# A task of the side work that wakes from a pause goes on only at every second group of weights

## The chip, the cores and the metric

The kernel runs on one core of one Trainium2 chip. The metric is the device time of one execution in microseconds (us). The profile is of one execution; its engines are PE (TensorE; PEld is its weight load), DVE (VectorE), ACT (ScalarE), POOL (GpSimd) and SP, whose queue issues nearly all the DMAs.

## What is computed

One inference step of a decoder with two layers, for 256 prompt tokens and 8 sequences of 4 new tokens, all in float32. Cut to what matters here, a layer is:

```python
g_cols, u_pool, u_conf, u_sc, q, k, v, qi, ki, wi = split_cols(x @ w_in)
a_out = pool_mixer(u_pool, ...)                       # sums over 2, 4, 8, 16 rows, then a small matmul
b_out = silu(layer_norm(causal_dwconv(ga * sigmoid(gb), ...)))     # 31 taps
c_out = sb * causal_dwconv(sc_ * sh, ...)             # 3 taps
d_out = attend(q, k, v, qi, ki, wi)                   # top-k of an indexer's scores, softmax over those keys
gates = sigmoid(g_cols)
merged = (gates[0] * (a_out @ w_br_pool) + gates[1] * (b_out @ w_br_conv)
          + gates[2] * (c_out @ w_br_sconv) + gates[3] * (d_out @ w_br_attn))
x1 = layer_norm(ALPHA * x + merged @ w_o)
r = ALPHA * x1 + (silu(hg) * hu) @ w_ffn_out          # hg, hu = x1 @ w_ffn_in
y = layer_norm(r + (pe @ w_pe) * sigmoid(r @ w_pg))
```

The attention of the prompt (`attn_prompt`) and that of the new tokens (`attn_sample`), which reads pages of a cache of keys and values, together give `d_out`.

## The kernel before

Activations lie with features on the partitions: a tile of 128 features x 288 columns (256 prompt tokens and 32 new ones). A weight matrix is cut into tiles of 128x128, and eight of them, in the order of their use, make a **group** of 512 KB. There are 306 groups. Each weight is split into a rounded high part and a rest, and so is each activation; a tile of weights costs three matmuls (lines 292 to 294): high x high, high x rest, rest x high. A group is thus 24 matmuls of PE.

**The pipeline of the groups.** When PE's program comes to a new group g, `W` (line 278) calls `fetch`: SP issues the DMA of group g+5 into `wraw` (4 buffers), ACT makes `whi` of group g+3 (line 264, 4 buffers), DVE makes `wlo` of group g+2 (line 271, 3 buffers).

**The side work.** Behind `fetch`, `W` calls `side`, which advances a counter, `tick`, and lets the tasks go on. A task is a Python generator that emits instructions: `conv`, `sconv`, `pool`, `index_prompt`, `index_sample`, `attn_prompt`, `attn_sample`. The instructions stand in each engine's order where the generator emitted them, all at this point between two groups. A task yields a pair (microseconds of DVE, of ACT), which is taken from the budget of this tick (1.96 and 2.3 us), or a whole number n, a **pause**: it goes on n ticks later at the earliest. The task does so where its next instruction needs the result of another engine, and also where it waits for a buffer of `b` or a bank `ax`. `conv` alone is low: it goes on where no other task can. Each engine works through its own order strictly, so what the side work emits on PE stands between the matmuls of two groups.

**Where a task must be done.** `layer` calls `finish` for a task whose result comes next. It steps that task until it is done, and at every advance of the tick each other task too that has no pause left, with no budget and with no group of weights in between. In a layer the order around this is: `qkv`, the projections for the other mixers, gates 0 and 2, `finish(pool)`, branch pool, `finish(sconv)`, branch sconv, gates 1 and 3 (16 projections of 8 weight tiles: one group each), then `finish` of the index and attention tasks, `pe_load` (a DMA, then a split by ACT at line 327 and DVE at line 328), branch attn, `finish(conv)`. A branch takes 4 groups and its outputs are multiplied by a gate on DVE (lines 1057 and 1060), out of 4 PSUM buffers `mm`.

**The end of the attention tasks**, which the prediction follows. `attn_prompt`, second block: scores masked (line 837) and their maximum (842), eight Exp on ACT (849), normalised on DVE (856), four rounds of four transposes on PE (868), each copied by ACT (870), the product with the values (880), copied by ACT (884), its rest on DVE (887). `attn_sample`, second half (f = 1): pages of keys by 8 DMAs of 256 KB (913) into `kv`, scores on PE (976, 979, 983), maximum on DVE (988), 8 DMAs for the values, Exp (994), three transposes (1002, 1003), copied by ACT (1005, 1006), the product with the values (1011, 1014), scaled on DVE (1018), four small matmuls that gather the heads (1027), copied by ACT (1032), the rest on DVE (1035). Both write `dp`, which the first matmul of branch attn reads.

Of the kernel before, what the change touches and what calls it, by code (L numbers as in the profile page):

```python
# [109 lines left out]
class Task:  # L110
    def __init__(self, gen, low):
        self.gen, self.wake, self.done, self.low, self.needs = gen, 0, False, low, BOTH


class Builder:
# [74 lines left out]
    def step(self, t):  # L190
        try:
            r = next(t.gen)
        except StopIteration:
            t.done = True
            self.tasks.remove(t)
            return
        if isinstance(r, int):
            t.wake = self.tick + r
        elif r is VECTOR or r is BOTH:
            t.needs = r  # L200
        else:
            self.left[0] -= r[0]
            self.left[1] -= r[1]

    def side(self):
        self.tick += 1
        for i in range(2):
            self.left[i] = min(self.left[i], 0.0) + self.budget[i]
        can = lambda t: not t.done and t.wake <= self.tick and all(self.left[i] > 0 for i in t.needs)
        while True:  # L210
            ready = [t for t in self.tasks if can(t)]
            if not ready:
                break
            ready = [t for t in ready if not t.low] or ready
            for t in ready:
                if can(t):
                    self.step(t)
# [674 lines left out]
    def load_kidx(self):  # L892
        nc, l, d = self.nc, self.l, self.d
        self.kx = self.sb.tile([128, 4, 2, 128], F32, name="kv", tag="kv", bufs=4)
        rows = slice(PHYS * l, PHYS * (l + 1))
        for b in range(NB):
            for g in range(2):
                i = 2 * b + g
                if i not in self.page:
                    self.page[i] = nc.sync.value_load(self.pt[0:1, i:i + 1], min_val=0, max_val=PHYS - 1)  # L900
                nc.sync.dma_start(self.kx[64 * (b % 2):64 * (b % 2) + 64, b // 2, g],
                                  d["kidx"][rows][ds(self.page[2 * b + g], 1)].rearrange("a p k -> p (a k)"))
                yield 0, 0.01
            yield 1

    def load_pages(self, which, f):
        nc, l, d = self.nc, self.l, self.d
        rows = slice(PHYS * l, PHYS * (l + 1))
        out = []
        for b in range(4 * f, 4 * f + 4):  # L910
            t = self.sb.tile([128, 2, 4, 128], F32, name="kv", tag="kv", bufs=4)
            for g in range(2):
                nc.sync.dma_start(t[:, g].rearrange("p c k -> p (c k)"),
                                  d[which][rows][ds(self.page[2 * b + g], 1)].rearrange("a p k -> p (a k)"))
            out.append(t)
        yield 1
        return out

    def index_sample(self):
# [520 lines left out]
```

## Time and profile before

| | |
|---|---|
| time, median of 3 runs | 1084.68 us (1083.91 to 1085.72) |
| the profiled execution | 1083.62 us, of which the span of the trace is 1081.8 us |
| PE busy | 1066.2 us, 99% of the span |
| PE weight load busy | 1030.5 us, 95% |
| DVE, ACT, POOL busy | 770.9, 557.5, 174.4 us (71%, 52%, 16%) |
| DMA | 188.58 MB, 174 GB/s |

A matmul's shown time is that of its way through the pipeline; what a matmul costs is the distance between two starts. The number in brackets behind a row is the idle time of its engine just ahead of it, and what ended it. Lines are those of the kernel before; in the changed kernel the lines named here and below stand 6 lower (line 880 is 886 there).

### The profile page before, as it was taken

To read this page: it belongs to the slowest core of one execution; us is meant where nothing else is said; L and a number is where in the kernel's file an instruction comes from. 1 tells how busy PE (TensorE), PEld (TensorE's weight loads), DVE (VectorE), ACT (ScalarE), POOL (GpSimd) and SP (SyncE) were. 2 spreads that over 40 slices of the span, in tenths; PEclk is the share of its full clock that TensorE was granted. 3 is DMA by queue.
4 is the path that set the end of the run, shared out by engine and by line. 5 is a ranking of instruction groups with operands and counts; after the bars stand their busy time and mean duration, and the time that the engine had idled before them with its cause. 6 is when DMAs were issued, how large, how long until landed. Compare 5 with 4: busy or idle time off the path is not lost.

```text
span 1081.8 us, 20642 instructions
## 1 busy us (share of the span) xinstructions
PE 1066.2 (99%) x8138; PEld 1030.5 (95%) x8138; DVE 770.9 (71%) x1305; ACT 557.5 (52%) x930; POOL 174.4 (16%) x175
## 2 busy tenths in 40 slices
PE   9999999999999999999999999999999999999996
PEld 8999989999999999999999998899999999999995
DVE  5898858678785555545789897687698765555456
ACT  5866445455564444434578565363545644443334
POOL 0720003005500000000437100030055000000004
PEclk9999999999999999999999999999999999999998
DMA  9476566344445555554445856563453644554541
GB/s 320 153 260 205 180 238 212 115 163 150 153 156 176 156 172 169 166 160 166 167 151 176 283 175 211 195 212 119 152 168 118 196 159 163 173 171 159 173 137 44
DMA packets 61732, 188.58 MB, mean 174 GB/s; under 512 B 7587, under 2 KB 12227, under 8 KB 61635
## 3 DMA queue, kind: packets, MB, share of 16 engines
q1 hardware_dynamic: 60498, 183.54, 51.5%
q0 software_dynamic: 992, 3.57, 0.9%
q8 instruction: 64, 1.05, 0.4%
q14 instruction: 34, 0.27, 0.1%
q10 hardware_dynamic: 144, 0.15, 0.1%
HBM read 182.48 MB, written 4.75 MB: 173 GB/s over the span
## 4 chain that ended last, share of the span: by engine, by line
PE 91%; DVE 4%; ACT 2%; POOL 2%; issue 1%; DMA 0%; SPq 0%; DVEq 0%; POOLq 0%; ACTq 0%
PE mm L292 24%; PE mm L293 24%; PE mm L294 24%; PE mm L319 2%; PE mm L321 2%; PE mm L315 2%; DVE wlo L271 1%; PE ax L293 1%; PE ax L292 1%; PE ax L294 1%; PE ax L321 1%; POOL b L341 1%; PE ax L319 1%; PE ax L315 1%; POOL b L372 1%
## 5 line engine op out<-in xcount | busy, mean ns | idle before, releaser
L271 DVE TENSOR_TENSOR wlo<-wraw,whi 128x1024 fp32r<-128x1024 f32 (+1 forms) x309 | 384.4, 1246 | 144.6 <-issue 79.6
L292 PE MATMUL mm<-xh,whi 128*128 128x288 f32 x1536 | 455.3, 296 | 0.8 <-DVE s L1060 0.8
L294 PE MATMUL mm<-xh,wlo 128*128 128x288 f32 x1536 | 453.1, 295 | 0.9 <-DVE wlo L271 0.8
L293 PE MATMUL mm<-xl,whi 128*128 128x288 f32 x1536 | 453.2, 295 | 0.0
L264 ACT ACTIVATE whi<-wraw 128x1024 fp32r<-128x1024 f32 (+1 forms) x309 | 322.6, 1046 | 152.3 <-PE mm L293 80.7
L292 PEld LDWEIGHTS mm<-xh,whi 128*128 128x128 f32 x1536 | 288.8, 188 | 8.6 <-issue 7.4
L294 PEld LDWEIGHTS mm<-xh,wlo 128*128 128x128 f32 x1536 | 288.6, 188 | 1.7 <-DVE wlo L271 1.6
L293 PEld LDWEIGHTS mm<-xl,whi 128*128 128x128 f32 x1536 | 288.8, 188 | 0.4
L292 PE MATMUL mm<-b,whi 128*128 128x288 f32 x576 | 171.8, 298 | 0.0
L293 PE MATMUL mm<-b,whi 128*128 128x288 f32 x576 | 169.9, 295 | 0.0
L294 PE MATMUL mm<-b,wlo 128*128 128x288 f32 x576 | 169.5, 294 | 0.0
L292 PEld LDWEIGHTS mm<-b,whi 128*128 128x128 f32 x576 | 107.9, 187 | 0.9 <-issue 0.4
L294 PEld LDWEIGHTS mm<-b,wlo 128*128 128x128 f32 x576 | 108.5, 188 | 0.0
L293 PEld LDWEIGHTS mm<-b,whi 128*128 128x128 f32 x576 | 108.1, 188 | 0.3
L1061 POOL TENSOR_TENSOR m<-m,s 128x288 f32<-128x288 f32 x32 | 38.2, 1226 | 273.5 <-DVE s L1060 273.5
L339 POOL TENSOR_TENSOR b<-xf 128x288 f32<-128x288 f32 x4 | 4.9, 1220 | 443.5 <-DVE xf L1206 434.8
L1179 ACT ACTIVATE b<-s 128x288 fp32r<-128x288 f32 x44 | 19.3, 445 | 92.1 <-DVE s L1174 92.1
L682 DVE SCALAR_TENSOR_TENSOR b<-b,prm 128x256 f32<-128x256 f32 x120 | 63.1, 573 | 0.0
L1174 DVE TENSOR_TENSOR s<-s,mm 128x288 f32<-128x288 f32 x40 | 18.0, 454 | 50.4 <-PE mm L294 50.4
L1045 ACT ACTIVATE xf<-mm 128x288 f32<-128x288 f32 x32 | 13.2, 412 | 63.0 <-PE mm L294 63.0
L1045 ACT ACTIVATE g<-mm 128x288 f32<-128x288 f32 x32 | 13.2, 412 | 60.2 <-PE mm L294 60.1
L1182 DVE TENSOR_TENSOR b<-s,b 128x288 fp32r<-128x288 f32 x44 | 19.8, 458 | 19.4 <-ACT b L1179 19.4
(252 smaller groups left out, 1235.1 us busy)
## 6 DMA issues: line engine op xcount, KB each, us to landing
wraw<-in_w_dram SPq DMA_DIRECT2D x304, 512.0 KB, 3.5
kv<-in_ck_dram SPq DMA_DIRECT2D x32, 256.0 KB, 5.3
kv<-in_cv_dram SPq DMA_DIRECT2D x32, 256.0 KB, 4.8
out_ko_dram<-b POOLq DMA_DIRECT2D x2, 576.0 KB, 5.0
out_vo_dram<-b POOLq DMA_DIRECT2D x2, 576.0 KB, 7.2
kv<-in_kidx_dram SPq DMA_DIRECT2D x32, 32.0 KB, 3.1
b<-in_p_dram SPq DMA_DIRECT2D x3, 288.0 KB, 4.0
wraw<-in_w_dram SPq DMA_DIRECT2D x3, 256.0 KB, 4.8
```

The source lines that it names most:

```text
L264: self.nc.scalar.activation(self.hi[g][:, c[i]], self.raw[g][:, c[i]], AF.Copy)
L271: self.nc.vector.tensor_tensor(self.lo[g][:, c[i]], self.raw[g][:, c[i]], self.hi[g][:, c[i]].bitcast(F32), op=OP.subtract)
L292: m(out, wh, rh, start=first, stop=False)
L293: m(out, wh, rl, start=False, stop=False)
L294: m(out, wl, rh, start=False, stop=last)
L315: m(o, wh, rh[:, k], start=k == 0, stop=False)
L319: m(o, wh, rl[:, k], start=False, stop=not early and k == nk - 1)
L321: m(o, wl, rh[:, k], start=False, stop=False)
L682: nc.vector.scalar_tensor_tensor(o, e, wj, o, op0=OP.mult, op1=OP.add)
L1045: self.nc.scalar.activation(g, a, AF.Sigmoid)
L1061: nc.gpsimd.tensor_tensor(self.m[:, j], self.m[:, j], t, op=OP.add)
L1182: nc.vector.tensor_tensor(h[:, 1, i % 2], t, h[:, 0, i % 2].bitcast(F32), op=OP.subtract)
```

## The change

A pause that ends at an odd tick is lengthened by one tick: a task other than `conv` that has yielded a whole number goes on only at an even one. The same holds for a task that polls for a buffer. A pair as a yield is not touched, and neither is `finish`, which looks at the pause alone. The pauses behind the page DMAs are excepted: they yield 1.0 in place of 1, a float, for which the mark is not set.

```diff
 class Task:
     def __init__(self, gen, low):
         self.gen, self.wake, self.done, self.low, self.needs = gen, 0, False, low, BOTH
+        self.turn = False
...
-        if isinstance(r, int):
-            t.wake = self.tick + r
+        t.turn = isinstance(r, int) and not t.low
+        if isinstance(r, (int, float)):
+            t.wake = self.tick + int(r)
...
-        can = lambda t: not t.done and t.wake <= self.tick and all(self.left[i] > 0 for i in t.needs)
+
+        def can(t):
+            return (not t.done and t.wake <= self.tick and all(self.left[i] > 0 for i in t.needs)
+                    and not (t.turn and self.tick % 2))
...
@@ load_kidx and load_pages
-            yield 1
+            yield 1.0
```

Instructions of the same kinds and sizes stand in another order; two more loads of ACT's function table are the only new ones on a compute engine. On PE the side work stood in 48 places between the weight matmuls and stands in 43 now. Three places follow.

PE, first layer, between gate 3 and branch attn. Rows whose input is `xh` or `xl` are the end of gate 3, rows with input `b` the start of branch attn. Before:

```order
L292 MATMUL mm<-xh,whi 128x288
L293 MATMUL mm<-xl,whi 128x288
L294 MATMUL mm<-xh,wlo 128x288
L292 MATMUL mm<-b,whi 128x288
L293 MATMUL mm<-b,whi 128x288
L294 MATMUL mm<-b,wlo 128x288
```

The same place now:

```order
L298 MATMUL mm<-xh,whi 128x288
L299 MATMUL mm<-xl,whi 128x288
L300 MATMUL mm<-xh,wlo 128x288
L874 MATMUL ax<-const_214,b 128x128 x4
L1008 MATMUL ax<-const_214,rls 128x128 x2
L1009 MATMUL ax<-const_214,rls 32x128
L886 MATMUL ax<-b 64x128 x16
L1017 MATMUL ax<-vs,pst 128x512
L1020 MATMUL ax<-kv,pst 32x512 x8
L1033 MATMUL ax<-const_214,b 128x16 x4
L298 MATMUL mm<-b,whi 128x288
L299 MATMUL mm<-b,whi 128x288
```

The last round of transposes of `attn_prompt` and the whole end of `attn_sample` moved here; they stood 12 to 15 groups earlier. The second layer has the same rows at this place, with eight transposes in place of four and with L886 ahead of L1008.

ACT, second layer, the same place: L1045 (L1051 now) is the sigmoid of a gate, L327 (L333) the split of `pe_load`. Before:

```order
L1045 ACTIVATE g<-mm 128x288
L264 ACTIVATE whi<-wraw 128x1024
L730 ACTIVATE s<-b 128x288 x2
L1045 ACTIVATE g<-mm 128x288
L327 ACTIVATE b<-b 128x576
L264 ACTIVATE whi<-wraw 128x1024
```

Now:

```order
L1051 ACTIVATE g<-mm 128x288
L876 ACTIVATE b<-ax 128x512 x2
L736 ACTIVATE s<-b 128x288
L890 ACTIVATE b<-ax 128x4x128
L736 ACTIVATE s<-b 128x288
L1011 ACTIVATE pst<-ax 128x256
L1012 ACTIVATE pst<-ax 32x128
L1038 ACTIVATE b<-ax 128x4x16
L333 ACTIVATE b<-b 128x576
L270 ACTIVATE whi<-wraw 128x1024 x2
```

The copies that PE's rows at this place need stand between the sigmoid of the last gate and the split, with a sigmoid of `conv` (L736) among them.

ACT, first layer, the eight Exp of the second block of `attn_prompt`. Before, in the branches pool and sconv, where ACT has no gate to work on:

```order
L264 ACTIVATE whi<-wraw 128x1024 x2
L849 ACT_TABLE_LOAD
L849 ACTIVATE b,st<-b,st 128x256 x8
L264 ACTIVATE whi<-wraw 128x1024 x2
L994 ACTIVATE rls,sts<-ax,sts 128x288
```

Now, in gate 1:

```order
L1051 ACTIVATE xf<-mm 128x288
L270 ACTIVATE whi<-wraw 128x1024
L855 ACT_TABLE_LOAD
L855 ACTIVATE b,st<-b,st 128x256 x8
L1051 ACT_TABLE_LOAD
L1051 ACTIVATE xf<-mm 128x288
L270 ACTIVATE whi<-wraw 128x1024
```

They moved 7 groups down the program, out of the branches; in the second layer they move by as much.

## Rows read from the trace of the kernel before

**Rows 1.** The page: busy time of PE, and the chain that ended last, by engine.
```profile
PE 1066.2 (99%) x8138; PEld 1030.5 (95%) x8138; DVE 770.9 (71%) x1305; ACT 557.5 (52%) x930; POOL 174.4 (16%) x175
...
PE 91%; DVE 4%; ACT 2%; POOL 2%; issue 1%; DMA 0%; SPq 0%; DVEq 0%; POOLq 0%; ACTq 0%
```

**Rows 2.** Timeline of PE (start us, us, engine, line): two rows 116 matmuls apart.
```profile
244.78 0.29 PE L293 MATMUL mm<-b,whi 128*128 128x288 f32 x1
...
260.25 0.30 PE L292 MATMUL ax<-b,whi 128*128 128x288 f32 x1
```

**Rows 3.** Timeline of PE: blocks of side work in both layers.
```profile
192.31 1.09 PE L868 MATMUL ax<-const,b 128*128 128x128 f32 x8
...
729.98 0.60 PE L868 MATMUL ax<-const,b 128*128 128x128 f32 x4
730.33 0.39 PE L292 MATMUL mm<-xh,whi 128*128 128x288 f32 x1
730.55 0.30 PE L293 MATMUL mm<-xl,whi 128*128 128x288 f32 x1
...
733.69 1.97 PE L880 MATMUL ax<-b 128*64 128x128 f32 x32
735.59 1.12 PE L1011 MATMUL ax<-vs,pst 32*128 32x512 f32 x2
...
738.50 0.40 PE L292 MATMUL mm<-xh,whi 128*128 128x288 f32 x1
...
741.77 0.96 PE L1027 MATMUL ax<-const,b 128*128 128x16 f32 x8
742.58 0.38 PE L292 MATMUL mm<-xh,whi 128*128 128x288 f32 x1
```

**Rows 4.** Timeline of the other engines: copies and scalings of the attention tasks.
```profile
140.39 0.59 ACT L870 ACTIVATE b<-ax 128x512 f32<-128x512 f32 x1
140.87 0.38 ACT L1005 ACTIVATE pst<-ax 128x256 f32<-128x256 f32 x1
141.13 0.25 ACT L1006 ACTIVATE pst<-ax 32x128 f32<-32x128 f32 x1
...
202.34 0.22 DVE L1035 TENSOR_TENSOR b<-ax,b 128x64 fp32r<-128x64 f32 x1
...
735.71 0.60 ACT L884 ACTIVATE b<-ax 128x512 fp32r<-128x512 f32 x1 [0.55 <-PE ax L880]
738.71 0.75 DVE L1018 SCALAR_TENSOR_TENSOR b<-ax,sts,const 128x512 f32<-128x512 f32 x1 [3.63 <-PE ax L1014]
743.23 0.21 ACT L1032 ACTIVATE b<-ax 128x64 fp32r<-128x64 f32 x1
```

**Rows 5.** Timeline of PE: the pages' first use (first layer, f = 1).
```profile
148.90 0.96 PE L1027 MATMUL ax<-const,b 128*128 128x16 f32 x8
...
161.83 0.75 PE L976 MATMUL ax<-scs,const 32*128 32x288 f32 x2
...
163.52 1.93 PE L983 MATMUL ax<-kv,qbd 128*32 128x256 f32 x32
```

**Rows 6.** The tile kv on SP from 150 to 156 us: its eight DMAs.
```profile
L913 SPq DMA_DIRECT2D kv<-in_ck_dram x8: 332/333/463, 151.0 to 154.8; - x8
DMA to landing us min/median/max: 3.5/5.0/5.4
```

**Rows 7.** Timeline: ends of branch sconv, first and second layer.
```profile
182.11 0.37 PE L292 MATMUL mm<-xh,whi 128*128 128x288 f32 x1 [0.26 <-DVE s L1060]
...
715.32 1.79 DVE L271 TENSOR_TENSOR wlo<-wraw,whi 128x1024 fp32r<-128x1024 f32 x1 [0.42 <-ACT whi L264]
...
718.18 0.37 PE L292 MATMUL mm<-xh,whi 128*128 128x288 f32 x1 [0.58 <-DVE s L1060]
```

**Rows 8.** Windows: stretch, us, busy (xinstructions) by engine, granted clock, DMA share, GB/s.
```profile
1070.00:1074.00 4.00, 2.31 (x34) 1.58 (x34) 2.00 (x6) 2.01 (x6) 1.30 (x3) 1.00 0.01 4
1074.00:1078.00 4.00, 0.33 (x3) 0.13 (x2) 3.74 (x11) 2.97 (x6) 2.65 (x4) 0.51 0.28 100
```

More of the change, by code (lines that the diff above doesn't have):

```diff
@@ L915, in load_pages @@
             out.append(t)
-        yield 1
+        yield 1.0
         return out
```

## The prediction

> **What bounds the kernel now.** I read the page first: PE is busy for 99% of the span, and of the chain that ended last 91% is PE [rows 1]. No other engine is near that. So what counts is what stands in PE's order, and where PE stands still.
>
> Next the pace of that order. Two matmuls of the stream that are 116 apart start 15.47 us apart [rows 2], so one weight matmul costs 0.1334 us, a group of 24 costs 3.20 us, and the 7344 of the program (306 groups) some 980 us. About 100 us of the 1081.8 are left for side work on PE, layer norms, start and end.
>
> Then single blocks of side work. Four transposes hold the stream for 0.35 us (729.98 to 730.33), and the weight matmul behind them takes 0.22 us to the next start in place of 0.13: 0.09 us for leaving a block. The product with the values takes 1.90 us for the prompt (733.69 to 735.59) and 2.91 for the sample (735.59 to 738.50), the four gathering matmuls 0.81 (741.77 to 742.58) [rows 3]. None of these rows carries a wait: ACT's and DVE's answers are ready when PE comes to the next step, because at least one group of 3.2 us lies between.
>
> **The change, part by part.** *Work.* No matmul, and no instruction that computes on DVE or ACT, is added or taken away; two more loads of a function table run on ACT (52% busy [rows 1]) beside the stream. What changes is when a task goes on. A pause that would end at an odd tick costs one group more, and the chain of pauses of an attention task gets longer by many of these. Before, both attention tasks are done some 10 groups before `finish` asks for them, in each layer. Now they aren't, and the rest comes out in one piece, between gate 3 and branch attn. There PE has nothing else in its order. I call this piece the tail.
>
> *The tail, second layer.* I follow PE from the first of the eight transposes (t = 0). Eight are busy for 1.09 us, four for 0.60, so eight hold PE for 0.35 + 0.49 = 0.84 us [rows 3]. ACT has the sigmoid of the last gate ahead (done by then), and two copies of 512 columns: 0.59 us each, the next instruction starting 0.48 later [rows 4]. From an end to a start on another engine I take 0.06 us (the product's last end at 735.66 [rows 3], ACT's copy at 735.71 [rows 4]). First copy from 0.66, second from 1.15 to 1.74, PE on at 1.80, free at 0.84: wait 0.96. The prompt's product takes 1.90, to 3.70, then three transposes about 0.24, to 3.94. ACT copies the product from 3.82, has a sigmoid of `conv` next (an estimate: 0.34, between the 0.26 to the next start of a 256-column copy and the 0.48 of a 512-column one), then the copies of the three transposes, 0.26 and 0.25 [rows 4], done at 5.15, PE on at 5.21: wait 1.27. The sample's product takes 2.91, to 8.12. DVE starts the scaling 0.21 behind that (738.50 to 738.71) and takes 0.75 [rows 3, 4]; PE on at 9.14: wait 1.02. The gathering takes 0.81, to 9.95, its end shows 0.15 later [rows 3]; ACT's copy takes 0.21 and then DVE's rest 0.22 [rows 4]: first weight matmul at 10.4, the second held by 0.15 more: wait 0.63. Together 3.9 us.
>
> *The tail, first layer.* Four transposes and the three of the sample fill 0.59 us; ACT's copy is done at 1.25, PE goes on at 1.31: wait 0.72. ACT copies for the sample while the product runs, so there is no second wait. Scaling and gathering as above: 1.02 and 0.63. Together 2.4 us.
>
> Both tails: 6.3 us. From below: scaling and gathering have no other PE work beside them by the order, 2 x (1.02 + 0.63) = 3.3. From above: every copy in full behind its matmul, none overlapped with PE or with another: 5.4 and 3.6, so 9. I take 6.3, since each piece has its row.
>
> *Behind the tail.* PE's wait holds up branch attn alone. On DVE there queue behind the scaling the rest of dp, the split of `pe_load`, and `wlo` of the group two ahead; that weight is needed 6.4 us after the tail's end, so I cost it at nothing. Without that cover it would be the 1.8 us that such a `wlo` once took [rows 7]. The DMA of `pe_load` stands in SP's queue ahead of weights that are due five groups later.
>
> *The pages of keys, first layer (f = 1).* A block begins at 148.90, at the start of the group ahead of the page DMAs [rows 5]. The last of these is issued at 154.8 and lands at most 5.4 later [rows 6], so 11.3 us behind that group's start. PE needs them at 163.52, 14.6 behind it, because blocks of side work lie between [rows 5]. Now three bare groups do, 9.6 us, and the 1.7 us of lines 976 and 979 (161.83 to 163.52): 11.3. The slack is gone, and the eight Exp of `attn_prompt`, now a few groups earlier in gate 1, may set ACT back, and with it `wlo` and SP. I take 0.5, between 0 and 2. In the second layer blocks still lie between: 0.
>
> *Waits that may go.* At the end of branch sconv PE stands 0.26 us in the first layer and 0.58 in the second, for DVE, which itself stood 0.42 for a late `whi` of ACT [rows 7], behind the eight Exp. These leave this stretch. First layer: DVE has no more beside the branch than before, so -0.35 with the slow restart of 0.09. Second layer: maskings of scores and a maximum move into the branches, and the last step of `pool` stands nearer to its branch: I take no change, between -0.7 and +1.5.
>
> *Fewer blocks.* 43 for 48: five times 0.09 = -0.45, between 0 and -1.0 (if entering costs as much as leaving).
>
> *Sum.* 6.3 + 0.5 - 0.35 - 0.45 = +6.0 us. The profiled execution took 1083.62 us, 1.06 below the median of the three runs; 6.0 on the median gives **1090.7 us** (1089.6 for an execution like the profiled one).
>
> **A rule weighed.** From 1070 to 1074 us PE is busy for 2.31 of 4 us and the granted clock is still 1.00 (2.4 GHz); in the next 4 us, with 0.33 busy, it is 0.51 (1.2 GHz) [rows 8]. In the tails PE works for some 7 of 11 and 6 of 9 us, so by the rows the clock holds. The Trainium skill, "TensorE: Matmul & The Clock Gate", section "Why this matters for your kernels", asks that there be no long idle gaps between bursts of matmuls, since the clock then falls back; it speaks against a chain of waits in one place, and what a fall would give is rival B.
>
> **The rivals.**
> A. *The tail costs only what the order forces.* ACT's copies are done when PE comes to them, so that scaling and gathering alone stall: 3.3 us. With both branch waits gone (-1.0) and the full 1.0 for the blocks the net is +1.3: 1086.0, not slower by what can be told. For it: ACT is idle for half of the span [rows 1]. Against: in the second layer ACT's chain is longer than the PE work beside it, by rows. It decides where the tails come to under 4.2 us and the gains reach their far ends.
> B. *The clock falls in the tails.* At the low level a weight matmul takes twice its 0.133 us. If that lasts for the 4 us of the low window [rows 8], 15 matmuls take 2 us more, at both tails 4: 1094.7. Against it: the window before that.
> C. *DVE's queue becomes the next wait.* Behind the scaling stand a split and a `wlo`; if these hold up the reading of the branch's outputs as in branch sconv now (0.58 [rows 7]), and the pages come late too, that is 1.5 to 3 more: 1093. For it: DVE stands still through much of the tail with its queue behind it.
> D. *The gains outweigh.* Entering and leaving a block costs far more than 0.09, which no row shows. It would take over 1.5 us per block against the tails: 1082.
>
> **How the numbers follow.** About 0.2% (2.2 us) is what a measurement of this kernel can tell from no change. Forecast 0.76, A 0.09, B 0.05, C 0.07, D 0.03. The predicted time is the forecast's, 1090.7. Its unknown terms reach from +1.3 to +12.5; I leave out the ends, where several terms would have to lie at their bounds at once: 1087.0 to 1094.8. Slower: forecast, B and C, less the forecast's lowest part, 0.87; same: A and that part, 0.10; faster 0.03.
>
> **What would show it.** In the trace of the changed kernel: a block of PE between gate 3 and branch attn in each layer, some 9 and 11 us long, with waits of PE for ACT's line 876 (0.7 and 1.0), ACT's 1012 in the second layer (1.3), DVE's 1024 (1.0 each) and ACT's 1038 (0.5 each); no wait of PE at the end of branch sconv in the first layer; at most 2 us of wait for `kv` at line 989 in the first layer; granted clock 1.00 throughout. I am wrong if PE's waits in the tails sum to less than 4.5 us, if a new wait of over 1.5 us stands outside the tails, or if the stream's pace of 0.133 us changes.

## The result, and the profile after

The changed kernel takes 1095.44 us (median of four runs, 1092.84 to 1097.63), the kernel before 1084.51 beside it: a ratio of 1.0098, 95% interval 1.0075 to 1.0122, so slower by 10.9 us. The forecast was 1090.7 in a range of 1087.0 to 1094.8: the direction was right, the size was not. The profiled execution took 1095.4, with a span of 1093.6, which lies at the median. One execution of an experiment below, of 1283.1 us at a mean granted clock of 0.76, is left out of its median. The runs of one kernel lie up to 5.6 us apart, so a difference of two medians below is good to one or two us; the sizes of single places come from the traces.

First the page of the kernel after: busy time by engine, and the chain, as in [rows 1].

```profile
PE 1072.8 (98%) x8138; PEld 1034.2 (95%) x8138; DVE 769.7 (70%) x1305; ACT 561.3 (51%) x932; POOL 174.8 (16%) x175
...
PE 87%; ACT 3%; DVE 3%; DMA 2%; issue 2%; POOL 2%; SPq 1%; POOLq 0%; DVEq 0%; ACTq 0%
```

As many matmuls as before (x8138) and two table loads more on ACT; but PE is busy for 6.6 us longer, and DMA, 0% of the chain before, has 2%. What PE waited for, from the view of waits (instruction, what it waited for: us in all, times, longest):

```profile
PE ax L989 <- DMA kv<-in_ck_dram: 2.0, 3, 0.9
PE ax L1033 <- DVE b L1024: 1.9, 2, 1.0
PE ax L886 <- ACT b L876: 1.2, 1, 1.2
PE ax L1017 <- ACT pst L1012: 1.0, 1, 1.0
...
PE mm L298 <- ACT b L1038: 0.6, 2, 0.3
```

The last four are the tails, at the lines that the prediction named. The first is the pages of keys, to which it gave 0.5 us. The tails themselves, second layer (from the eight transposes) and then first layer, timeline of PE:

```profile
778.28 1.03 PE L874 MATMUL ax<-const,b 128*128 128x128 f32 x8
779.25 0.44 PE L886 MATMUL ax<-b 128*64 128x128 f32 x4
780.84 1.75 PE L886 MATMUL ax<-b 128*64 128x128 f32 x28 [1.15 <-ACT b L876]
...
784.03 1.12 PE L1017 MATMUL ax<-vs,pst 32*128 32x512 f32 x2 [0.96 <-ACT pst L1012]
...
787.95 1.07 PE L1033 MATMUL ax<-const,b 128*128 128x16 f32 x8 [0.95 <-DVE b L1024]
789.33 0.40 PE L298 MATMUL mm<-b,whi 128*128 128x288 f32 x1 [0.31 <-ACT b L1038]
789.59 0.40 PE L299 MATMUL mm<-b,whi 128*128 128x288 f32 x1
789.83 0.29 PE L300 MATMUL mm<-b,wlo 128*128 128x288 f32 x1
```

```profile
240.27 0.60 PE L874 MATMUL ax<-const,b 128*128 128x128 f32 x4
...
240.92 0.27 PE L1009 MATMUL ax<-const,rls 128*32 128x128 f32 x1
241.13 1.97 PE L886 MATMUL ax<-b 128*64 128x128 f32 x32
...
246.95 1.06 PE L1033 MATMUL ax<-const,b 128*128 128x16 f32 x8 [0.95 <-DVE b L1024]
248.33 0.40 PE L298 MATMUL mm<-b,whi 128*128 128x288 f32 x1 [0.31 <-ACT b L1038]
```

Next the product with the pages for f = 1, first layer and second. Before, in the first layer, it was one piece of 1.93 us with no wait [rows 5]; now it stands twice for `kv` and takes 6.0 us, 211.88 to 217.88:

```profile
211.88 1.03 PE L989 MATMUL ax<-kv,qbd 128*32 128x256 f32 x4
213.72 0.99 PE L989 MATMUL ax<-kv,qbd 128*32 128x256 f32 x2 [0.81 <-DMA kv<-in_ck_dram]
214.98 2.97 PE L989 MATMUL ax<-kv,qbd 128*32 128x256 f32 x26 [0.27 <-DMA kv<-in_ck_dram]
217.88 1.24 PE L708 MATMUL ax<-b,const 128*128 128x288 f32 x4
...
760.74 0.63 PE L989 MATMUL ax<-kv,qbd 128*32 128x256 f32 x6
762.25 1.89 PE L989 MATMUL ax<-kv,qbd 128*32 128x256 f32 x26 [0.88 <-DMA kv<-in_ck_dram]
```

And the granted clock (windows; the number behind POOL's is the clock). Before it was 1.00 from start to end, but for the last microseconds [rows 8]:

```profile
212.00:216.00 4.00, 2.92 (x18) 0.96 (x21) 2.50 (x10) 0.00 (x0) 0.00 (x0) 0.72 1.03 412
216.00:220.00 4.00, 4.00 (x34) 2.68 (x26) 0.46 (x1) 0.00 (x0) 0.00 (x0) 0.85 0.42 169
786.00:790.00 4.00, 2.74 (x24) 1.66 (x17) 1.82 (x5) 0.94 (x3) 0.00 (x0) 1.00 0.00 0
790.00:794.00 4.00, 4.00 (x21) 4.00 (x21) 2.24 (x3) 0.80 (x1) 0.80 (x1) 0.58 0.27 74
```

Ahead of its end the program had two falls of the clock to the lower level (1.2 GHz, 0.5): in the wait for the pages, and just behind the second tail, where branch attn is already running: 21 matmuls instead of some 30 in 4 us. Their starts there (timeline of PE):

```profile
791.08 0.45 PE L299 MATMUL mm<-b,whi 128*128 128x288 f32 x1
791.32 0.45 PE L300 MATMUL mm<-b,wlo 128*128 128x288 f32 x1
```

In the pages the fall costs too: the 26 matmuls behind the last landing show 2.97 us in the first layer, and 1.89 in the second, where the clock was 1.00.

**Where the time went.** All kernels here have the same 7344 weight matmuls in the same order, so the start of the n-th in one trace can be subtracted from its start in another. The differences say, group by group, where a kernel falls behind the kernel before. In us, for the changed kernel and three experiments told below:

| stretch (groups of 24 weight matmuls) | after | pages early | no Exp | filled |
|---|---|---|---|---|
| start, 0 to 24 | -0.22 | +0.70 | +0.62 | +1.59 |
| first layer, 24 to 72 | +5.72 | +3.10 | +3.29 | +1.57 |
| of it the group with the pages f = 1 | 8.64 | 4.50 | 4.68 | 4.50 |
| of it the tail, with the group behind it | 8.29 | 9.82 | 9.81 | 8.29 |
| second layer, 168 to 238 | +5.66 | +6.62 | +2.69 | +2.71 |
| of it the group with the pages f = 1 | 5.65 | 4.19 | 4.19 | 4.18 |
| of it the tail, with the group behind it | 12.80 | 15.21 | 11.28 | 11.28 |
| program | +11.24 | +10.45 | +6.61 | +5.91 |

(The lines "of it" hold work that before stands elsewhere, so only their differences from column to column count.) Pages: 8.64 - 4.50 = 4.14 in the first layer, 5.65 - 4.19 = 1.46 in the second, 5.6 in all. The fall of the clock behind the second tail: 12.80 - 11.28 = 1.5. What is left is the tails net of all gains: 5.72 - 4.14 = 1.58 and 5.66 - 1.46 - 1.52 = 2.68, 4.3 in all. With the start's -0.2 that makes 11.2. The 4.14 of the first layer's pages are 3.0 of lateness (the last load lands at 214.84, PE is there at 211.88) and 1.1 of the clock (2.97 - 1.89).

### The profile page after: what moved, and what is told of

Same layout as the page of the kernel before. It is cut to its first block, busy times and chain, and to the rows that moved or that the text cites. A ratio compares the mean times of both kernels' runs of the same rounds, so it can differ in the third digit from the quotient of the medians.

```text
span 1093.6 us, 20646 instructions
## 1 busy us (share of the span) xinstructions
PE 1072.8 (98%) x8138; PEld 1034.2 (95%) x8138; DVE 769.7 (70%) x1305; ACT 561.3 (51%) x932; POOL 174.8 (16%) x175
## 4 chain that ended last, share of the span: by engine, by line
PE 87%; ACT 3%; DVE 3%; DMA 2%; issue 2%; POOL 2%; SPq 1%; POOLq 0%; DVEq 0%; ACTq 0%
PE mm L298 23%; PE mm L299 23%; PE mm L300 23%; PE mm L325 2%; PE mm L327 2%; PE mm L321 2%; DMA kv<-in_ck_dram 1%; PE ax L299 1%; DVE wlo L277 1%; PE ax L298 1%; PE ax L300 1%; PE ax L989 1%; POOL b L347 1%; ACT whi L270 1%; PE ax L327 1%
## 5 line engine op out<-in xcount | busy, mean ns | idle before, releaser
L1051 ACT ACTIVATE g<-mm 128x288 f32<-128x288 f32 x32 | 13.2, 413 | 52.1 <-PE mm L300 52.0
L1051 ACT ACTIVATE xf<-mm 128x288 f32<-128x288 f32 x32 | 13.2, 411 | 42.1 <-PE mm L300 42.1
```

The lines of the kernel that those rows point to most:

```text
L1051: self.nc.scalar.activation(g, a, AF.Sigmoid)
```

## The experiments

**How the pages come late.** ACT in the changed kernel, timeline from a `whi` over the eight Exp of the prompt's second block (their last ends at 197.9) to the next `whi`; then DVE, and SP's eight loads:

```profile
191.57 1.05 ACT L270 ACTIVATE whi<-wraw 128x1024 fp32r<-128x1024 f32 x1
192.64 1.28 ACT L855 ACT_TABLE_LOAD   x1
...
198.01 1.28 ACT L1051 ACT_TABLE_LOAD   x1
199.30 0.41 ACT L1051 ACTIVATE xf<-mm 128x288 f32<-128x288 f32 x1
199.61 1.05 ACT L270 ACTIVATE whi<-wraw 128x1024 fp32r<-128x1024 f32 x1
```

```profile
200.69 1.23 DVE L277 TENSOR_TENSOR wlo<-wraw,whi 128x1024 fp32r<-128x1024 f32 x1 [3.39 <-ACT whi L270]
```

```profile
205.49 4.11 SPq L919 DMA_DIRECT2D kv<-in_ck_dram  x8
```

In the kernel before, the same Exp stood in branch sconv, where ACT has no sigmoid in its queue:

```profile
173.00 1.28 ACT L849 ACT_TABLE_LOAD   x1
...
178.25 1.99 ACT L264 ACTIVATE whi<-wraw 128x1024 fp32r<-128x1024 f32 x2
```

There the Exp held ACT for 5.25 us and two `whi` followed at once. In gate 1 a sigmoid stands between, with a table load of its own: 6.97 us from 192.64 to the next `whi`. The Trainium skill, "ScalarE: Activation LUTs", section "Table sets: the hidden batching unit", has it that functions come in sets and that changing the set costs a load; the trace agrees, at 1.28 us each. `wlo` needs `whi`, the buffer of raw weights is free only behind `wlo`, and SP's weight loads wait for that buffer with the loads of `kv` behind them: last issue 209.27, landing 4.1 to 5.6 us after the issue, the last at 214.84, while PE is there at 211.88. Theory: late pages and tails cost, and the clock falls behind such waits. Two experiments take the pages' lateness away in different ways.

*Pages early.* In `attn_sample`:

```
             nc.tensor.matmul(...)                 # last readers of kv for f = 0
+            if not f:
+                early = self.pages("ck", 1)       # eight DMAs issued here
...
-                kt = yield from self.load_pages("ck", f)
+                kt = early
+                yield 1.0
```

> The changed kernel, but the eight DMAs for the second half's pages of keys are put into SP's queue right behind the matmuls that read the buffers last (the values of the first half), some 10 groups earlier; the order on PE, ACT and DVE is unchanged. Theory 1 (two causes: late pages cost about 4.2 us in the first layer and 1.6 in the second with the fall of the clock that follows them, the tails some 6 us and 1.6 for the clock): no wait for the pages is left, the two blocks that hold them fall from 8.6 and 6.4 us to about 4.4 and 4.7, the tails stay at 8 and 11 us, the time falls by 5 to 6 us, to 1089 to 1090.5. Rival (the pages are late because DMA bandwidth is short there, and what is moved away comes back as late weights): the time falls by less than 2 us and PE waits for wlo instead.

Measured: 1091.17 (1088.32 to 1093.96), ratio 1.0057 (1.0036 to 1.0078), 4.3 us less than the changed kernel. No wait for `kv` is left, and the group with the pages costs 4.14 and 1.46 us less in the two layers. The profiled execution, the longest of the four, shows why no more came of it (windows over the second tail):

```profile
784.00:788.00 4.00, 2.86 (x16) 1.78 (x8) 1.49 (x3) 0.18 (x2) 0.00 (x0) 0.50 0.00 0
788.00:792.00 4.00, 3.90 (x16) 3.90 (x17) 2.58 (x4) 1.57 (x3) 0.00 (x0) 0.50 0.16 26
```

Here the clock fell inside the tail and stayed at 0.50 into branch attn: 15.21 us in place of 11.28. It fell behind the first tail as well: 9.82 in place of 8.29. Over its four runs the mean granted clock and the time go together: 0.997 twice (1088.3, 1089.4), 0.993 (1092.9), 0.991 (1094.0). So the tails net of the gains, without a fall of the clock, cost some 4 us.

*No Exp.* In `attn_prompt`, both layers:

```
-            for h in range(8):
+            if i:
+                nc.vector.memset(st[:, 1], 1e30)  # row sums of the second block
+            for h in range(8 if i == 0 else 0):
```

> The changed kernel without the eight Exp of the second block of the prompt's attention, in both layers (the sums of the rows are set to a constant, so the output isn't the reference's); the order of all else is unchanged. Theory 1 (in the first layer the Exp, now in gate 1, make ACT late with whi, so DVE with wlo, so SP with the weights that stand ahead of the pages): SP issues the pages some 2 us earlier against PE, PE's wait for them in the first layer falls from about 3.6 us to under 1.5 and the clock stays up there; the second layer, where the Exp lie further ahead, keeps its wait of 1.5. The time falls by 2.5 to 4.5 us, to 1091 to 1093. Rival (the distance of two bare groups alone is too short for the burst of eight DMAs, whatever ACT does): the wait stays over 2.5 us and the time within 1.5 us of the changed kernel.

Measured: 1090.38 (1089.10 to 1092.93), ratio 1.0063 (1.0045 to 1.0080), 5.1 us less. No wait for `kv` in either layer; in the first the loads go out from 203.4 on, in an execution whose stream stands 0.84 later there, so 2.9 us earlier against the stream than in the changed kernel; in the second they go out 1.8 us earlier against it. The product with the pages is one piece again:

```profile
212.72 2.11 PE L991 MATMUL ax<-kv,qbd 128*32 128x256 f32 x32
```

That settles the chain from the Exp to the pages. It was stronger than expected: the second layer's wait went too.

**The rule without tails.** Two experiments let the attention tasks end in time.

*Rule not for attention:*

```
-        t.turn = isinstance(r, int) and not t.low
+        t.turn = (isinstance(r, int) and not t.low
+                  and t.gen.__name__ not in ("attn_prompt", "attn_sample"))
```

> The rule of the change for all tasks but the two attention tasks. These then are done before they are asked for (one group ahead in both layers), so there is no tail. Theory 1 (only the attention tasks' lateness costs): no waits of PE for lines 876, 1012, 1024, 1038, the time within 2 us of the kernel before, 1083 to 1086.5; the pages again have two groups from issue to use, with a wait of 0 to 2 us. Rival (the rule costs by piling up DVE and ACT work at even ticks, whichever task it is): 1089 or more with waits of PE for wlo.

Measured: 1095.08 (1092.62 to 1096.89), ratio 1.0094 (1.0077 to 1.0111). A miss: no tail, and as slow as the changed kernel; by the aligned streams it is 7.7 us behind in the first layer and 6.4 in the second. The trace shows two things that this edit made itself. The attention tasks now run ahead of the index tasks, which keep the rule. In the second layer SP stands in the first loads of keys until the index product, delayed by the rule, has read the pages in the same four buffers; the weights queue behind them (view of the tile, then ACT's timeline and PE's waits):

```profile
L919 SPq DMA_DIRECT2D kv<-in_ck_dram x8: 332/338/857, 615.0 to 629.9; - x8
L938 PE MATMUL ax<-kv,qibd x8: 378/390/404, 628.6 to 628.8; 128*32 128x256 f32 x8
```

```profile
637.44 1.06 ACT L270 ACTIVATE whi<-wraw 128x1024 fp32r<-128x1024 f32 x1 [11.53 <-DMA wraw<-in_w_dram]
```

```profile
PE ax L989 <- DMA kv<-in_ck_dram: 2.8, 3, 1.0
...
PE mm L298 <- ACT whi L270: 2.1, 1, 2.1
```

And the pages for f = 1 still stand behind the Exp. The clock fell in both layers behind such waits (0.50 from 210 to 214 us and from 640 to 644). So the run doesn't say that tails are free; it says that these late loads cost as much.

*Rule off from gate 3 on*, so that the rest of attention is spread over gate 3:

```
+        self.free_turn = True                     # in layer(), ahead of gate(3)
         self.gate(3)
...
-                    and not (t.turn and self.tick % 2))
+                    and not (t.turn and self.tick % 2 and not self.free_turn))
```

> The changed kernel, with the rule switched off from the start of gate 3 on, 8 groups before the attention tasks are asked for. The same steps as in the tails come out between the groups of gate 3; the four gathering matmuls alone still stand in front of branch attn. Theory 1: PE's waits for 876, 1012 and 1024 are gone, 0.5 us per layer for 1038 stays, the clock doesn't fall in front of branch attn, the waits for the pages stay as they were or get smaller by the transposes that now stand ahead of them. The time falls by 5 to 8 us, to 1087.5 to 1090.5. Rival (the tails are a minor part and the pages are nearly all of it): it falls by less than 3 us.

Measured: 1091.54 (1088.99 to 1092.44), ratio 1.0065 (1.0048 to 1.0081), 3.9 us less, where 5 to 8 were expected: the tails are gone but for the gathering, the pages are still late (waits 0.67 and 0.66), the clock falls behind that wait in the first layer, and a new wait of PE stands in the first layer, 1.29 us for DVE's scaling of the prompt's rows (L863) at 212.09.

*Both edits at once*, the two diffs above together:

> The changed kernel with both earlier edits at once: the pages of keys for f=1 are issued right behind the last readers of their buffers, and the rule is off from the start of gate 3, so that the attention tasks are all but done before branch attn. Theory (the loss is made of late pages and of tails, and each group of waits in one place can also pull the granted clock down; nothing else costs): the two savings add up, 4.3 and 3.9 of the 10.9 us, and the falls of the clock go with the waits. Left are the four gathering matmuls in front of branch attn (0.6 in each layer) and the wait of the first layer's transposes for DVE seen with the rule off in gate 3 (1.3), less the branch waits and blocks that are gone (about 0.8): 1084 to 1087 us, all runs within 2 us of each other, granted clock 1.00 in every stretch but the last one of the program. Rival (the rule costs by itself, in every pause, wherever the tasks end): at least 1088. Second rival (the clock falls whatever the waits are, in this order of tasks): the lowest run near 1085, but runs spread over 4 us as in the changed kernel.

Measured: 1088.09 (1086.20 to 1090.27), ratio 1.0033 (1.0020 to 1.0045). The savings nearly add up, 7.4 of the 10.9 us in place of 8.2, and the median is 1.1 above the expectation's upper end; the clock did not stay at 1.00 either. By the aligned streams the second layer is now at +0.4, the first at +3.6. There stand the wait for L863 and, right behind it, the clock:

```profile
PE ax L875 <- DVE b L863: 1.3, 1, 1.3
```

```profile
212.00:216.00 4.00, 3.87 (x30) 2.36 (x34) 2.97 (x9) 0.69 (x2) 0.00 (x0) 0.82 0.43 135
216.00:220.00 4.00, 4.00 (x40) 2.58 (x33) 0.00 (x0) 1.09 (x2) 0.00 (x0) 0.75 0.59 168
```

The two windows lose 0.18 x 4 + 0.25 x 4 = 1.7 us of full clock; with the wait that is 3.0 of the 3.6. The rule by itself, away from these places, costs no more than about 1 us by the streams; the first rival (at least 1088) is met by the median, but not by the place of its cost.

**What the clock costs.** *Tails filled:* the kernel with the pages early, and matmuls that nobody reads where PE waits in the tails (7 behind the second layer's transposes of either task, 7 behind the sample's product and 3 behind the gathering in both layers):

```
+    def fill(self, n):
+        if self.fin:                              # only inside finish()
+            a = self.mm()
+            for _ in range(n):
+                self.nc.tensor.matmul(a[:, :N], self.xl[:, 0, :128], self.xh[:, 0],
+                                      start=True, stop=True)
```

> The kernel with the pages early (tails as in the changed kernel), and in each tail matmuls of 288 columns that nobody reads stand where PE waits: 7 behind the second layer's transposes of the prompt and of the sample, 7 behind the sample's product and 3 behind the gathering in both layers, 34 in all, about 0.93 us for seven. They take the place of waits, so by themselves they should cost at most 0.5 us. Theory (waits in one place make the granted clock fall, and that alone spreads the runs): the clock stays at 1.00 in both tails, and all runs lie at 1088 to 1089.5, where the two quickest runs of the same kernel without filling lay (1088.3 and 1089.4), not at its median of 1091.2. Rival (the clock does not hang on PE's waits there): median still about 1091, runs spread over 5 us, stretches at 0.5 behind 245 and 780 us. Second rival (the matmuls come on top of the waits): up to 3.9 us more, 1092 to 1095.

Measured: 1088.18 (1087.67 to 1089.44), ratio 1.0035 (1.0022 to 1.0048). Thirty-four matmuls more, and 3.0 us less at the median than with the pages early alone, though the two intervals overlap; the runs lie within 1.8 us instead of 5.6, and their mean granted clock within 0.995 to 0.997 instead of 0.991 to 0.997. Timeline and windows of the second tail:

```profile
777.00 1.75 PE L895 MATMUL ax<-b 128*64 128x128 f32 x28 [0.23 <-ACT b L884]
...
778.98 1.17 PE L234 MATMUL mm<-xh,xl 128*128 128x288 f32 x7
780.19 1.12 PE L1032 MATMUL ax<-vs,pst 32*128 32x512 f32 x2
```

```profile
780.00:784.00 4.00, 3.96 (x27) 1.62 (x25) 0.81 (x3) 0.14 (x2) 0.00 (x0) 1.00 0.00 0
784.00:788.00 4.00, 4.00 (x32) 3.81 (x31) 2.97 (x7) 1.75 (x3) 0.00 (x0) 1.00 0.02 4
```

The waits are replaced by work, the tail takes as long as a tail with waits at full clock (11.28 in both), and the clock stays at 1.00. In each of the three traces with waits in both tails (changed kernel, pages early, no Exp) the clock fell in or behind a tail; in none of the four with filled tails (this one and three below) did it. So the clock falls because PE waits there.

*The changed kernel filled*, its pages late as they are: the same in the tails, and 20 and 8 unread matmuls ahead of the product with the pages; this kernel once more; and the tails alone. With `tail=False`, `fill` also works outside `finish`.

```
             for c in range(4):                    # matmuls of qbd with k
                 ...
+            if f:
+                self.fill(20 - 12 * self.l, tail=False)
             for c in range(4):                    # matmuls with the pages
```

> The changed kernel itself, its pages still late, with matmuls of 288 columns that nobody reads where PE waits: the 34 in the two tails, and ahead of the product with the pages of f=1 20 more in the first layer and 8 in the second. Theory (the granted clock falls behind PE's waits, and that is what lies between the changed kernel's clean sum and its median): no stretch at 0.5 before the program's end, so that the 1.7 us of the fall in the first layer's pages and the 1.5 us behind the second tail go, with some of the slow restarts: 1091 to 1092.5, all runs within 2.5 us. Rival (the late pages and the tails cost their time by the waits alone, or the clock falls all the same): 1094 to 1097, as the changed kernel.

> The changed kernel with tails and pages filled once more, since its runs lay in two groups (1092.8 and 1093.6, then 1095.6 twice) though the clock had not fallen in any. If the pages' landing varies from one execution to the next, a slow execution's trace shows the last of the kv loads landing later than in the quick one and PE standing behind the filling matmuls; if the start varies (PE's waits for wlo near 33 us), the difference is all there before 60 us. Time: 1093 to 1096 again.

> The changed kernel with its pages late as they are, and the 34 unread matmuls in the two tails alone. If the fall of the clock behind the tails is a cost of its own in the changed kernel (1.5 us in its profiled execution, up to 3.9 where the fall stood inside a tail), the median comes to 1092 to 1094, the stretch at 0.5 behind the second tail is gone, the one in the first layer's pages may stay. If filling gains nothing while the pages are late, 1095 to 1096.

Measured: 1094.64 and 1094.07 with both filled (1.0096, 1.0081 to 1.0111; and 1.0081, 1.0068 to 1.0094), 1093.46 with the tails alone (1.0078, 1.0066 to 1.0090). The first missed: the clock did not fall before the program's end, but its median is only 0.8 lower than the changed kernel's. By the medians against the kernel before measured beside each, filling the tails gave 2.6 us also here (8.3 above it, in place of 10.9), with overlapping intervals; by the aligned streams the second tail, with the group behind it, takes 11.29 in place of 12.80. Filling in front of the pages gave nothing on top by the medians (10.4 and 9.0 above the kernel before), since the pages are late all the same and the filling is fixed at 2.7 and 1.1 us; the pages' group in the first layer cost 7.34 and 7.99. In the profiled execution with filled tails alone that group cost 8.16, though the clock there was 1.00 throughout: lateness by itself can cost 8.16 - 4.50 = 3.7 us in that place, and how late the loads land differs from execution to execution.

The two profiled executions with all filled, of 1092.8 and 1095.5 us, differ by 2.1 us at the end of the stream, 1.3 of it before 60 us and 0.6 in the first layer's pages. The start's part is PE's wait for a `wlo` near 33 us: 1.32 and 2.02 in these two, 0.38 in the changed kernel, 0.44 before. Over all traces here it lies between 0.38 and 2.02, so a single execution says no more than about 2 us.

**Is there a better kernel?** What the Exp cost where they stood *before*: the kernel before without the second block's Exp (the edit as above), and with them in two halves.

> The kernel before without the eight Exp of the prompt's second block in both layers (their row sums are set to a constant instead, so the attention of that block is left out of what is computed). It says what these Exp cost where they stand before the change. Theory (there they cost the waits at the end of branch sconv alone, 0.3 and 1.3): 1 to 1.6 us less, 1082.5 to 1083.2. Rival (they cost nothing there): 1084. Against the changed kernel, where leaving the same Exp out gave 5.1 us, it tells how much of their price comes from the place to which the rule moves them.

Measured: 1083.28 (1082.31 to 1084.75), ratio 0.9992 (0.9983 to 1.0000): 1.0 us. So the rule raised the price of the same eight Exp from 1.0 to 5.1 us by moving them.

```
                 nc.scalar.activation(lg, lg, AF.Exp, ...)
-            yield 0, 2.56 + 8 * (0.3 + n / 1200)
+                if i and h == 3:
+                    yield 0, 2.56 + 4 * (0.3 + n / 1200)
+                    yield 1
+            yield 0, 2.56 + (8 - 4 * i) * (0.3 + n / 1200)
```

> The kernel before, with one edit: the eight Exp of the prompt's second block are written in two halves of four, a group of weights apart, so that ACT can convert a group of weights between them. Theory (the eight Exp in one piece hold up whi, and with it wlo, SP and PE): the waits of PE at the end of branch sconv (0.26 in the first layer, 0.58 and 0.75 in the second) go or shrink, 0.4 to 1.2 us less: 1083.0 to 1083.8. Rival (whi is late there for another reason, or the second half holds up the next weights in the same way): within 0.2 us of the kernel before, 1084.

> The kernel before with the eight Exp of the prompt's second block in two halves once more, to narrow the interval: the trace of its first run shows the waits at the end of branch sconv gone (0.25 in the first layer, 0.74 in the second), so 0.5 to 1.0 us less than the kernel before, 1083.3 to 1083.8. Rival: no difference, 1084.2.

Measured, eleven runs each: 1083.63, ratio 0.9994 (0.9985 to 1.0003), and 1083.33, ratio 0.9990 (0.9981 to 0.9999). The waits at the end of branch sconv in the second layer are gone; in the first one of 0.28 still stands in the second trace. By the aligned streams both traces gain 0.9 us in the second layer and nothing in the first. 0.6 and 0.9 us below the kernel before: the quickest version of this study that computes the same, by about what can be measured; one of the two intervals reaches 1.

## Why the prediction was right or wrong, step by step

- *The tails are the first cost, and where they stand:* right. Waits at the four lines named, between gate 3 and branch attn, and none elsewhere in them.
- *Second tail, 3.9 us (0.96, 1.27, 1.02, 0.63):* right in size: 1.15, 0.96, 0.95, and 0.31 with 0.24 for the slow second and third start, 3.6. The four are off by 0.3 at most, the first of them by luck. The prediction had the sigmoid of the last gate done by then and PE waiting for both copies; ACT loaded the sigmoid's table behind the sample's Exp, so the first copy started 1.9 us behind the first transpose, not 0.66, and PE went on as soon as that copy was done. The two errors cancel (ACT, timeline):

```profile
778.59 1.28 ACT L1051 ACT_TABLE_LOAD   x1
779.89 0.41 ACT L1051 ACTIVATE g<-mm 128x288 f32<-128x288 f32 x1
780.20 1.08 ACT L876 ACTIVATE b<-ax 128x512 f32<-128x512 f32 x2
```

- *First tail, 2.4 us:* 0.9 too high. The wait of 0.72 for ACT's copy didn't come: the product starts at 241.13, right behind the transposes. The four transposes that are left there are those of heads 4 to 7, and the product goes by pairs of heads, so it reads them only in its second half; the copy is done by then. The prediction took the product to need all four at its first matmul. The other two waits came as 0.95 and 0.55.
- *Branch waits:* gone in the first layer, as said. In the second the prediction took no change; the wait of 0.58 [rows 7] went as well, and the stream gains 0.66 us in that group.
- *Tails net of gains,* forecast 6.3 - 0.35 - 0.45 = 5.5: 4.3.
- *Pages of keys, first layer 0.5 (0 to 2), second 0:* **the step that failed**, 4.1 (3.0 of lateness and 1.1 of the clock) and 1.5. The mechanism was named for the first layer (Exp in gate 1, ACT, `wlo`, SP), but its price was taken, not worked out. The slack had been reckoned as gone already, so the whole delay had to come through: the Exp hold `whi` for 6.97 us, of which 1.28 are the return to the sigmoid's table, and 2.9 us of it reach the loads. In the second layer the prediction counted on the blocks in between; they give PE something to do, but 1.8 us of the delay reach the loads there too, more than the blocks cover.
- *The clock holds:* **failed too**; that was near to rival B, at 0.05. The clock fell in the wait for the pages and behind the second tail. B's price (2 us for 15 weight matmuls) was about right: 1.5 behind the second tail, 3.9 where the fall came inside a tail. What misled was the argument from one stretch, 2.31 of 4 us busy at 1.00 [rows 8]: in the changed kernel the last 4 us before the fall had 2.74 busy, also at 1.00, and the next stretch was at 0.58. The clock of a stretch tells what was granted in it, not what follows. Rows 8 say so themselves: with 0.51 as the mean of the 4 us from 1074 on, the clock can only have fallen at their very start, right behind the stretch with 2.31 of 4 us busy.
- *Rival C:* its late pages came, but by the Exp; of DVE's queue behind the scaling there is no sign, since with filled tails the group behind either tail takes 0.2 us longer than before, which is its slow start. *D:* no sign.

The sum by the forecast's own steps, with these sizes: 4.3 tails net, 5.6 pages (1.1 of it the clock), 1.5 clock behind the tail. The Trainium skill, "TensorE: Matmul & The Clock Gate", section "Why this matters for your kernels", asks for no long idle gaps between bursts of matmuls. The prediction read that as a warning against a chain of waits, and this reading was the better guide; but the page speaks of single long gaps, and the longest wait in the tails was 1.15 us.

What stays open: why the clock falls in one execution and not in another of the same kernel, and in which of several alike waits; the traces show where it fell, not what decides it. Nor was it traced why the landing of the pages and the wait near 33 us vary between executions.

## What to carry to other kernels

When a change delays a task, ask what its long instructions do to the queue that they now stand in: eight Exp that are cheap in one stage hold up conversion, then the buffers, then the DMA queue and its other loads in another. Where a load's slack is used up, price the whole delay, not a part. And several short waits of TensorE in one place can cost more than their sum, in work behind them that runs at the lower clock; unread matmuls in the waits of the tails got that back here.

## What the runs showed of the hardware that was not expected

- With waits of at most 1.15 us, and PE busy for 2.74 of the last 4 us, the granted clock went to 0.5 right behind the second tail; with 34 unread matmuls in the waits of the two tails it stayed at 1.00 in all four traces, and the kernel with the pages early took 3.0 us less at the median.
- At the lower clock a weight matmul starts 0.24 us after the one ahead (791.08 to 791.32), in place of 0.13; it is the work behind the waits that pays.
- The same kernel can differ by 5 us from one execution to the next, and time and clock go together: in the changed kernel 1092.8 at a mean granted clock of 0.995, and 1097.6 at 0.991. The kernel before stayed at 0.994 to 0.997, and within 3.2 us, in all of its runs.
